# Layer A's instruction order from the planner: gate products behind the next chunk's first tile, weights loaded ahead of x

## The chip, the cores and the metric

The kernel runs on one core of a Trainium2 chip. Five engines with an instruction queue each matter here: TensorE (PE, matmuls; its weight loads are listed as PEld), VectorE (DVE), ScalarE (ACT), GpSimd (POOL) and SyncE (SP, which here only issues transfers). The metric is the device time of one execution in microseconds (us), the median of several runs.

## The reference, cut to what matters

A trunk of two layers on x with 2048 positions and 1024 channels, in float32. Layer A is a recurrent layer, layer B attention with a window of 128.

```python
def rglru_layer(x, norm_g, w_in, conv_w, conv_b, wr, br, wi, bi, lam, w_out):
    h = rmsnorm(x, norm_g)
    u = h @ w_in                                   # 1024 -> 2 x 1536
    xb, gate = u[..., :LRU_WIDTH], u[..., LRU_WIDTH:]
    xb = causal_depthwise_conv(xb, conv_w, conv_b) # 4 taps along the sequence
    xs = xb.reshape(bsz, seq, LRU_BLOCKS, LRU_BLOCK_W)       # 16 blocks of 96
    r = sigmoid(einsum('bshi,hij->bshj', xs, wr) + br)
    i = sigmoid(einsum('bshi,hij->bshj', xs, wi) + bi)
    log_a = -LRU_C * r * softplus(-lam)
    a = exp(log_a)
    b = sqrt(-expm1(2.0 * log_a)) * (i * xb)
    hs = associative_scan(a, b)                    # h = a * h_before + b
    return x + (hs * silu(gate)) @ w_out           # 1536 -> 1024
...
x = rglru_layer(x, ...)
k, v = ...                                         # from rmsnorm(x) @ w_kv
x = swa_layer(x, k, v, ...)                        # q and gate projection, attention, out-projection
```

## The kernel before

**Numbers.** Each float32 operand of a matmul is split into a high and a low float16 half with a power-of-two scale, and a product is three passes (high x high, high x low, low x high; `PASSES`). The scale of a weight comes from the maximum over all of it: DVE reduces the maxima, and two small PE products (`f2_turn`, `f2_back`, together called floor2) spread them over the partitions. So a weight is loaded, its maximum taken, and then ACT makes the high half and DVE the low half (`split_flat`, lines 310 and 311).

**Layer A.** Width 1536 is cut into four groups (g) of three tiles of 128 channels; the sequence into four chunks (c) of 512 positions. One group and one chunk make a *unit*; the 16 units run group by group, and are numbered here u = 4 g + c, from 0 to 15. A unit has 144 matmuls of 512 columns in the x-branch (`pu`, three tiles of 24 matmuls in three passes) and the gate branch (`pg`), and 36 for the two gates r and i (`pr`). Per x-branch tile, ACT makes a copy `u` and a first tap `xc`, DVE adds three taps (line 535), ACT and DVE or POOL split the result into `hl` (lines 537, 538), and SP copies 32 of its rows into `b3` (line 540; the profile calls it b), which the gate products read. ACT then works through four tables: SiLU of `pg` (line 548), sigmoid of `pr` (line 567) and tanh, exp, sqrt. DVE does the recurrence as a scan (line 592), multiplies by SiLU, and POOL's queue stores the result y in DRAM (`yD`, line 602).

**Where things come from.** All products share six PSUM banks in a ring ("mm"). For each x block of 128 positions ACT squares it and sums (line 326), POOL raises the sum to the power -0.5 (line 318), and ACT and DVE split. The blocks of chunk 0 are turned by PE (`turn_x`, line 333), those of chunks 1 to 3 by a transposing DMA on SP (`flip`, line 341). They come through three load buffers and three for the halves, which lie in the memory of two of the four weight buffers ("W") until the last block is done. Weights pass through three staging buffers ("st"). `prep(g)` loads and splits the weights of group g while group g - 1 runs. After the units come 16 blocks of the out-projection (`out_block`: load y and x, split y, 72 matmuls `po`, add, store to `x1D`), beside which layer B's weights are prepared (`prep_B`, `prep_out`).

**What sets the order.** The order is that of the program text, which the tile framework's scheduler changes by priorities. In the text `unit` is a generator that stops after each tile; at each stop `run_side` advances the side work (`norm_chunk` for x, `prep` for weights, `w_out_prep` for the out-projection) by a fixed number of steps (`RATE`), with offsets on the priority (`LATE`, `AHEAD`). In a unit the order of the products is: three x-branch tiles, three gate-branch tiles, the two gates' products.

Layer B is written otherwise. Its work is a set of chains, generators that name the engine and the duration of the next step before they issue it, or a flag to wait for. `Plan.run` plays all chains against each other at build time, always issues the step that can begin first (then by rank), and the order that results on each engine is fixed by ties from each instruction to the one before it:

```python
yield ACT_, 1150                       # engine, duration in ns
act.activation(hi, xb, AF.Copy, scale=r10)
yield DVE_, 1280, 1                    # 1: shares a port with POOL
dve.scalar_tensor_tensor(lo, xb, r10, hi, ALU.mult, ALU.subtract)
if b >= 2:
    yield F["proj"][b - 2]             # a flag
```

Of the kernel before, what the change touches and what calls it, by code (L numbers as in the profile page):

```python
# [46 lines left out]
RATE = (3, 3, 3, 2)  # L47
LATE = (0, 0, 0, 300, -100, 200)
F2AHEAD = 200
LO_POOL = (1, 2)  # L50
AHEAD = (200, 200, 200)
# [5 lines left out]
ACT_, DVE_, POOL_, SP_ = range(4)  # L57
# [15 lines left out]
class Plan:  # L73
# [5 lines left out]
    def __init__(self):  # L79
        self.now = 0.0  # L80
        self.free = [0.0] * 4
        self.port = [0.0] * 4
        self.table = None
        self.asks = []
        self.n = 0
# [4 lines left out]
    def step(self, chain, rank, t):  # L90
# [13 lines left out]
        elif r is not None:  # L104
            self.n += 1
            self.asks.append((t, rank, self.n, chain, r))
# [13 lines left out]

    def run(self, streams):
        heads = [next(s, None) for s in streams]
        pe = 0.0
        while True:
            best = None
# [5 lines left out]
            ask = min(self.asks, key=lambda a: (self.begin(a), a[1], a[2]), default=None)  # L131
            if best is None and ask is None:
                break
            if ask is None or best is not None and best[0] <= self.begin(ask):
                t, i = best
                pe = t + heads[i][1]
                self.now = pe + (170 if heads[i][1] else 0)
                heads[i] = next(streams[i], None)
                continue
# [3 lines left out]
            if r[0] is not None:  # L143
# [6 lines left out]
                end += WAKE  # L150
            self.step(ask[3], ask[1], end)
# [4 lines left out]
def trunk(ctx, tc, x, wA, gw, par, gains, woA, wkv, wB, woB, vec, alib, out):  # L156
# [62 lines left out]
    def floor2(mx, n, keep):  # L219


        with tc.high_priority(offset=F2AHEAD):
            dve.tensor_copy(keep, f2_back(f2_round(f2_turn(mx, n), n), n))

    def floor2_apart(mx, n, keep, t1, t2):
# [14 lines left out]
    lastmm = [None]  # L240

# [10 lines left out]

    def conv_bounds():
        cabs = xp.tile([P, KR, 5], F32, name="cabs")
        dve.scalar_tensor_tensor(cabs, pr[:, :, 0:5], -1.0, pr[:, :, 0:5], ALU.mult, ALU.max)
        csum = xp.tile([P, KR], F32, name="csum")
        dve.tensor_reduce(csum, cabs[:, :, 0:4], AX.X, ALU.add)
        cmx = xp.tile([P, 2], F32, name="cmx")
        dve.tensor_reduce(cmx[:, 0:1], csum, AX.X, ALU.max)
        dve.tensor_reduce(cmx[:, 1:2], cabs[:, :, 4], AX.X, ALU.max)  # L260
        floor2(cmx, 2, cb2)

    def decay():

        nlam = xp.tile([P, KR], F32, name="nlam")
        lamv = pr[:, :, 7]
        dve.tensor_scalar(nlam, lamv, -1.0, None, ALU.mult)
        nal = xp.tile([P, KR], F32, name="nal")
        dve.tensor_tensor(nal, nlam, lamv, ALU.min)
        ee = xp.tile([P, KR], F32, name="ee")  # L270
        act.activation(ee, nal, AF.Exp)
        e2 = xp.tile([P, KR], F32, name="e2")
        dve.tensor_scalar(e2, ee, 2.0, None, ALU.add)
        e3 = xp.tile([P, KR], F32, name="e3")
        dve.reciprocal(e3, e2)
# [1263 lines left out]
```

## Time and profile before

| what | us |
|---|---|
| median of 3 runs (lowest, highest) | 1579.13 (1576.9, 1579.64) |
| the profiled execution's own time | 1580.0 |
| its span, from the first to the last instruction | 1578.3 |
| PE busy | 1510.0 (96%) |
| DVE, ACT, POOL busy | 1049.3, 881.2, 460.2 |
| mean granted clock of PE | 0.986 |

By stage: unit 0 begins its matmuls at 19.9 us and unit 1 at 74.06, the units end at about 652, the out-projection ends at 910.46, and layer B takes the rest. The profile names an operation by its line; all large matmuls are issued at line 246, so that they are told apart by what they write (`pu`, `pg`, `pr`, `po` in layer A; `pm`, `s` and again `po` in layer B). A matmul row's busy time is modelled and overlaps its neighbours, so matmul counts are priced by the time from one to the next in a long unbroken run.

### The profile page before, as it was taken

How to read it: one execution, taken by the hardware profiler on the slowest of the kernel's cores; microseconds unless marked ns; L12 is line 12 of the kernel's file. 1: busy time of each engine (PE TensorE's matmuls, PEld its weight loads, DVE VectorE, ACT ScalarE, POOL GpSimd, SP SyncE). 2: the span in 40 equal slices, each digit the busy share in tenths (PEclk: the TensorE clock that was granted, in tenths of full speed). 3: DMA queues.
4: the chain of work that ended last, by engine and by line, in shares of the span. 5: the costliest groups of instructions: out<-in, count | busy, mean ns of one | idle time of the engine just before them, and what ended most of it. 6: DMA issues, size and time to landing. Idle time of an engine off the chain costs nothing.

```text
span 1578.3 us, 23221 instructions
## 1 busy us (share of the span) xinstructions
PE 1510.0 (96%) x8575; PEld 752.1 (48%) x8575; DVE 1049.3 (66%) x2221; ACT 881.2 (56%) x1771; POOL 460.2 (29%) x578
## 2 busy tenths in 40 slices
PE   5889999999989999889999998999999999999987
PEld 4434444444434444334444455555555555555553
DVE  7667868866886666766256246666666666767675
ACT  5767667766666566620144145655555656556661
POOL 2243222222222232100000033444444444444431
PEclk9999999999999999999999999999999999999998
DMA  6663302100341120779358343454444444444333
GB/s 202 168 145 75 102 28 86 58 26 26 110 163 43 40 86 26 243 262 329 131 194 295 108 101 57 84 97 98 97 98 97 97 98 98 97 97 96 72 68 94
DMA packets 242546, 177.29 MB, mean 112 GB/s; under 512 B 205056, under 2 KB 215552, under 8 KB 242432
## 3 DMA queue, kind: packets, MB, share of 16 engines
q1 hardware_dynamic: 233984, 146.95, 35.9%
q0 software_dynamic: 8304, 28.84, 5.3%
q8 instruction: 67, 1.10, 0.3%
q14 instruction: 47, 0.39, 0.1%
q10 hardware_dynamic: 144, 0.01, 0.0%
HBM read 92.93 MB, written 29.36 MB: 77 GB/s over the span
## 4 chain that ended last, share of the span: by engine, by line
PE 81%; DVE 7%; DMA 5%; ACT 3%; issue 2%; POOL 1%; SPq 0%; ACTq 0%; POOLq 0%; DVEq 0%
PE pm L246 33%; PE po L246 17%; PE pu L246 13%; PE pg L246 11%; PE pr L246 4%; PE s L246 3%; DVE xc L535 1%; DMA wst<-in_woA_dram 1%; DMA xs<-in_x_dram 1%; DMA ppx<-gg 1%; DVE w L311 1%; DMA xnT<-in_wkv_dram 1%; DVE h L592 1%; DVE amx L299 0%; DVE ri L589 0%
## 5 line engine op out<-in xcount | busy, mean ns | idle before, releaser
L246 PEld LDWEIGHTS <-w 128*128 128x128 f16 x2520 | 234.1, 98 | 279.5 <-issue 17.6
L246 PE MATMUL pm<-wq,xT 128*128 128x512 f16 x1536 | 351.8, 379 | 0.0
L246 PE MATMUL pu<-xnT,w 128*128 128x512 f16 (+1 forms) x1368 | 258.7, 349 | 8.2 <-ACT ri L567 7.2
L246 PEld LDWEIGHTS <-xT 128*128 128x128 f16 x1920 | 187.4, 98 | 163.8 <-issue 0.7
L246 PE MATMUL po<-wo,xnT 128*128 128x512 f16 x1152 | 252.9, 382 | 6.2 <-DVE wo L311 5.2
L246 PE MATMUL pg<-xnT,w 128*128 128x512 f16 x1152 | 253.3, 379 | 2.8 <-ACT w L310 1.9
L246 PEld LDWEIGHTS <-xnT 128*128 128x128 f16 x1152 | 113.3, 98 | 144.5 <-issue 11.5
L246 PE MATMUL pm<-xnT,yT 128*128 128x512 f16 x768 | 173.4, 381 | 0.0
L535 DVE SCALAR_TENSOR_TENSOR xc<-u,cwS,xc 128x512 f32<-128x512 f32 x144 | 119.8, 835 | 29.2 <-ACT xc L533 27.9
L1326 ACT ACTIVATE sq<-sq,bi,ssc 128x128 f32<-128x128 f32 x256 | 124.0, 486 | 22.8 <-DVE bi L1323 22.8
L246 PEld LDWEIGHTS <-yT 128*128 128x128 f16 x768 | 74.5, 98 | 85.9 <-issue 1.9
L1310 DVE CUSTOM_DVE_ANT_0 sq<-sq,al 128x128 f32<-128x128 f32 x256 | 99.4, 433 | 1.6
L1301 DVE COPY_PREDICATED sq<-mask,s 128x256 f32<-128x256 int32 x128 | 56.5, 442 | 48.5 <-ACT sq L1299 47.5
L537 ACT CAST hl<-xc 128x512 f16<-128x512 f32 x48 | 29.5, 614 | 99.5 <-DVE xc L535 99.4
L310 ACT ACTIVATE xnT<-xnT,sy 128x1536 f16<-128x1536 f32 x16 | 25.0, 1571 | 105.9 <-PE po L246 105.9
L1299 ACT COPY sq<-s 128x256 f32<-128x256 f32 x128 | 47.5, 372 | 64.2 <-PE s L246 63.4
L587 DVE SCALAR_TENSOR_TENSOR ri<-xc,isig,ri 128x512 f32<-128x512 f32 x48 | 33.3, 749 | 72.6 <-ACT ri L567 72.6
L246 PE MATMUL s<-kT,qT 128*128 128x256 f16 x512 | 77.7, 275 | 1.6 <-DVE qy L1385 0.9
L246 PE MATMUL pr<-hl,gw 128*128 128x512 f16 x288 | 70.7, 390 | 7.1 <-ACT gs L548 7.1
L567 ACT ACTIVATE ri<-pr,pr,rsc 128x512 f32<-128x512 f32 x96 | 67.2, 775 | 16.2 <-PE pr L246 16.1
L530 POOL COPY uhist<-u 128x3 f32<-128x3 f32 x36 | 14.4, 401 | 210.4 <-ACT u L524 210.3
L1385 DVE TENSOR_TENSOR qy<-qy,po 128x256 f32<-128x256 f32 x64 | 26.8, 421 | 67.8 <-ACT qy L1383 67.6
(245 smaller groups left out, 2252.4 us busy)
## 6 DMA issues: line engine op xcount, KB each, us to landing
xnT<-in_wB_dram SPq DMA_DIRECT2D x32, 512.0 KB, 6.4
yD<-gs POOLq DMA_DIRECT2D x48, 256.0 KB, 2.7
wst<-in_woA_dram SPq DMA_DIRECT2D x24, 512.0 KB, 4.5
xnT<-yD SPq DMA_DIRECT2D x16, 768.0 KB, 5.3
st<-in_wA_dram SPq DMA_DIRECT2D x15, 768.0 KB, 5.0
xs<-in_x_dram SPq DMA_DIRECT2D x16, 512.0 KB, 4.6
xnT<-in_x_dram SPq DMA_DIRECT2D x16, 512.0 KB, 4.6
x1D<-xnT POOLq DMA_DIRECT2D x16, 512.0 KB, 4.6
```

What stands on the lines that cost most here:

```text
L246: lastmm[0] = pe.matmul(o, lhsT, rhs, start=start, stop=stop, skip_group_check=True)
L310: act.activation(hi, src, AF.Copy, scale=scale)
L311: dve.scalar_tensor_tensor(lo, src, scale, hi, ALU.mult, ALU.subtract)
L535: dve.scalar_tensor_tensor(xc, u[:, d : d + CH], cw[:, j, d : d + 1], xc, ALU.mult, ALU.add)
L537: act.copy(hl[:, 0], xc)
L567: act.activation(v, o[j], AF.Sigmoid, bias=pr[:, t, 5 + w : 6 + w], scale=W["rsc"])
L587: dve.scalar_tensor_tensor(i, xs[j], W["isig"], i, ALU.mult, ALU.mult)
L1299: act.copy(sl, o[:, :, P:])
L1301: dve.copy_predicated(sl, mask.unsqueeze(1).to_broadcast([P, 2, P]), o[:, :, 0:P])
L1310: dve.tensor_tensor_reduce(s[:, h], s[:, h], al[:, i * P : (i + 1) * P], 1.0, -3.4e38, ALU.add, ALU.max, m)
L1326: act.activation(s[:, h], s[:, h], AF.Exp, bias=d["bi"][:, h : h + 1], scale=ssc[:, h : h + 1], accum_out=d["lsum"][:, h : h + 1],)
L1385: dve.tensor_tensor(yv, yv, o[:, :, 0], ALU.add)
```

## The change

Layer A and the first two blocks of the out-projection become chains of one plan; layer B's chains are kept. What an instruction computes stays, and their number too. In parts:

- *The plan.* `Plan` gets PE as a fifth engine, so that the small floor2 products are asked for like other steps, a model of landing times (2.3 us and 2.7 ns per KB, one after another), and a choice by begin time plus 30 ns per rank in which a switch of ACT's table counts nothing. At its end every instruction is tied to the one before it on its engine. `high_priority`, `RATE`, `LATE` and `AHEAD` are gone from layer A.
- *Order of products.* A unit is: x-branch tile 0, then the gate products of the unit before it, x-branch tiles 1 and 2, then the gate branch. The last unit's gate products stand after its gate branch.
- *The head.* The two halves of group 0's x-branch weights are loaded first, then x blocks 0 to 3, then the parameters and the second weights. Unit 0's x-branch is computed in three pieces of x blocks (0), (1) and (2, 3), three tiles at a time, where it was four pieces of one block, and each product waits for its own half of x and its own weight slice.
- *x of chunks 1 to 3.* One chain normalizes the twelve blocks one after another; loads wait for the buffer of the block three before.
- *Weights.* `prep` of groups 1, 2, 3 begins at units 2, 5 and 8, and that of the out-projection at unit 11 (`PREP_AT`). A split is a step per slice on ACT that starts a step on DVE. Out-projection weights are loaded one ahead.
- *Out-projection.* Blocks 0 and 1 are in the plan. Layer B's preparation runs beside blocks 2 to 15, where it ran beside blocks 1 to 15.

```diff
+PREP_AT = (2, 1, 0, 3)
+FIRST = ((0, 1), (1, 2), (2, 4))
+OUT_PLANNED = 2
+WEIGHT = 30
+TABLE = 0
+RANKA = (2, 6, 6, 4, 5, 6, 2, 3, 4, 4, 6, 6)
...
+    def landing(kb):
+
+        t = max(plan.now + 2300, plan.dma) + kb * 2.7
+        plan.dma = t
+        return t - plan.now
...
+    def split_steps(src, scale, hi, lo, hif, lof, ns, rank):
+        yield ACT_, ns
+        act.activation(hi, src, AF.Copy, scale=scale)
+        hif.set()
+        plan.go(split_lo(src, scale, hi, lo, lof, ns), rank)
...
+    def products():
+        for u in range(NTRI * NCH):
+            g, c = divmod(u, NCH)
+            W = WS[g]
+            un = units[u]
+            yield [W["set0"]] + xn_f[c], 0
+            unit_f[u].set()
+            if u == 0:
+                o, fr = yield from proj_first(W)
+                for j in range(3):
+                    plan.go(inx(un, j, o[j], fr[j]), RANKA[0])
+            else:
+                for j in range(3):
+                    o, free = yield from proj(W, 0, j, c, "pu")
+                    plan.go(inx(un, j, o, free), RANKA[0])
+                    if j == 0:
+                        yield from gates(units[u - 1])
+            if c == NCH - 1:
+                W["free0"].set()
+            yield [W["set1"]], 0
+            for j in range(3):
+                un.pg[j] = yield from proj(W, 1, j, c, "pg")
+                un.pg_f[j].set()
+            if c == NCH - 1:
+                W["free1"].set()
+        yield from gates(units[-1])
+        for b in range(OUT_PLANNED):
+            yield from out_products(b)
...
+    def ring_loads():
+        for p in range(NB - 4):
...
+                yield xfree[p - 3]
+            yield SP_, 450
+            load_x(1 + p // 4, p % 4, xb0[X_RING[p % 3]])
...
+    def norm_chain():
+        for p in range(NB - 4):
...
+            yield xload[p]
+            xb, t = xb0[X_RING[p % 3]], xb0[HL_RING[p % 3]].bitcast(F16)
+            hi, lo = t[:, 0:D], t[:, D : 2 * D]
+            r10 = yield from norm_steps(xb, lo)
+            yield ACT_, 1150
+            act.activation(hi, xb, AF.Copy, scale=r10)
+            yield DVE_, 1285, 1
+            dve.scalar_tensor_tensor(lo, xb, r10, hi, ALU.mult, ALU.subtract)
+            xfree[p].set()
+            plan.go(norm_flip(p, c, b, t), RANKA[7])
...
+    begin_plan()
+    plan.go(first_weights([Fetch([P, 4, 384], wsrc(0, 0, h), 0) for h in range(2)]), FIRST_RANK[0])
+    plan.go(first_loads(), 1)
...
+    plan.run([products()])
+    end_plan()
...
-    for b in range(NB):
+    for b in range(OUT_PLANNED, NB):
         for _ in out_block(b):
-            run_side(side, 2 if b else 0, LATE[5])
+            run_side(side, 2, LATE5)
```

More of the change, by code (lines that the diff above doesn't have):

```diff
@@ new lines, in trunk, with take @@
+    py, sy, cA = (xp.tile([P, NCH], F32, name=n) for n in ("py", "sy", "cA"))
+    plan = Plan(True, WEIGHT, TABLE)
+    flag = lambda: Flag(plan)
+    rings = {}
+    BUFS = dict(W=4, st=3, mm=6, tp=2, u=3, xc=4, hl=4, b3=2, gs=4, ri0=4, ri1=4, q=3, h=2, gw=2, f2=1)
+    def take(tag):
+        r = rings.setdefault(tag, [])
+        f = None
+        while len(r) >= BUFS[tag] and r[-BUFS[tag]] is not f:
+            f = r[-BUFS[tag]]
+            yield f
+        r.append(flag())
+        return r[-1]
@@ new lines, in together, with floor2_steps @@
+    def together(flags, then):
+        for f in flags:
+            yield f
+        then.set()
+    def floor2_steps(mx, n, keep, slack=300):
+        lock = yield from take("f2")
+        free = yield from take("tp")
+        if slack:
+            yield None, slack
+        yield PE_, 160
+        tp = f2_turn(mx, n)
+        yield DVE_, 700
+        dg = f2_round(tp, n)
+        free.set()
+        free = yield from take("tp")
+        if slack:
+            yield None, slack
+        yield PE_, 300
+        bp = f2_back(dg, n)
+        yield DVE_, 170
+        dve.tensor_copy(keep, bp)
+        free.set()
+        lock.set()
@@ new lines, in first_turn @@
+    def first_turn(b, w, src, fl):
+        free = yield from take("tp")
+        tp = pst([P, KD, P], F16, "tp", uniq("xt"), BUFS["tp"])
+        yield PE_, 620
+        for k in range(KD):
+            pe.transpose(tp[:, k], src[:, k * P : (k + 1) * P], id16)
+        dest = xnV[0][:, w, :, b * P : (b + 1) * P]
+        if w == 0:
+            yield ACT_, 1000
+            act.copy(dest, tp)
+        else:
+            yield DVE_, 690
+            dve.tensor_copy(dest, tp)
+        free.set()
+        fl.set()
+        (x_lo if w else x_hi)[b].set()
@@ L750, in trunk @@
-    drain(w_out_prep(3))
-    dve.tensor_scalar(cA[:, 0:2], py[:, 0:2], pwo, 2.0**-28, ALU.mult, ALU.mult)
+        wo_scaled.set()
+        for k, ld in enumerate(wo_loads(rank)):
+            if k % 3 == 0:
+                yield from take("W")
+                wo.append(wtile(uniq("wo")).rearrange("p a (k c) -> p a k c", k=3))
+            yield ld.landed
+            w, lo = wo[-1], wo_f[k]
+            yield from split_steps(ld.t, swo, w[:, 0, k % 3], w[:, 1, k % 3], flag(), lo, WO_NS, RANKA[10])
+            plan.go(together([lo], ld.free), 0)
@@ L792, in out_block, with ahead @@
         pool.dma_start(x1D[b], xb)
+    def ahead(loads, n):
+        q, loads = [], list(loads)
+        for _ in range(len(loads)):
+            while len(q) <= n and loads:
+                q.append(loads.pop(0)())
+            yield q.pop(0)
     stg = [0]
```

961 lines of the change are left out of this document (606 added, 355 removed).

## The prediction

> **What bounds it now.** First the page's busy times, then the busy time of each engine by stage (columns: stretch, length, busy us and instructions of PE, PEld, DVE, ACT, POOL, then granted clock, DMA share, GB/s):
>
> ```profile
> PE 1510.0 (96%) x8575; PEld 752.1 (48%) x8575; DVE 1049.3 (66%) x2221; ACT 881.2 (56%) x1771; POOL 460.2 (29%) x578
> ...
> 0.00:20.00 20.00, 3.71 (x29) 3.24 (x30) 11.55 (x30) 11.99 (x17) 5.46 (x21) 1.00 0.86 318
> 20.00:45.80 25.80, 21.65 (x335) 20.32 (x333) 22.94 (x69) 15.65 (x26) 4.00 (x10) 1.00 0.54 133
> 45.80:74.06 28.26, 22.42 (x109) 8.79 (x110) 19.25 (x34) 20.32 (x31) 7.33 (x13) 1.00 0.54 131
> 110.50:124.00 13.50, 5.66 (x21) 1.68 (x20) 1.52 (x2) 8.35 (x12) 2.16 (x7) 0.66 0.96 198
> ...
> 197.76:345.58 147.82, 147.82 (x729) 65.19 (x728) 110.73 (x177) 97.59 (x143) 39.18 (x50) 1.00 0.17 52
> 345.58:419.00 73.42, 73.42 (x362) 32.53 (x363) 52.77 (x88) 49.47 (x72) 18.46 (x25) 1.00 0.17 51
> 419.00:463.55 44.55, 40.54 (x193) 17.14 (x185) 36.65 (x56) 26.12 (x39) 11.24 (x15) 0.92 0.38 125
> ...
> 610.60:652.00 41.40, 38.44 (x190) 16.93 (x188) 33.32 (x47) 30.86 (x39) 10.59 (x8) 0.98 0.33 106
> 652.00:690.00 38.00, 32.29 (x136) 13.82 (x135) 30.35 (x40) 18.84 (x23) 2.79 (x4) 0.93 0.74 243
> 690.00:910.46 220.46, 220.46 (x1025) 100.09 (x1024) 103.90 (x116) 52.33 (x48) 8.52 (x17) 1.00 0.62 219
> 910.46:1578.30 667.84, 646.37 (x4225) 359.56 (x4222) 442.97 (x1301) 381.26 (x1086) 273.15 (x304) 0.99 0.43 91
> ```
>
> PE is the bound: 96% of the span, and where it never idles two units (a unit is one group g and one chunk c) take 73.42 us, 36.7 each. So a gain can only come from PE's idle time: 1578.3 - 1510.0 = 68.3 us, of which 667.84 - 646.37 = 21.5 lie in layer B, whose chains keep their order. The rest, 46.8, lies in six places: 16.3 before 20 us, 4.2 and 5.8 in unit 0, 7.8 in unit 1, 4.0 in unit 10, 3.0 in unit 15 and 5.7 at the start of the out-projection. Idle PE also runs on slowly (clock 0.66, 0.92, 0.93 in those rows), so the full loss of a place is its length less its matmuls at full rate.
>
> The timeline shows what those waits end on (start, length, engine and line, in brackets the idle time before and its releaser):
>
> ```profile
> 4.25 1.06 ACT L326 ACTIVATE xri<-xs 128x1024 bf16<-128x1024 f32 x1 [1.73 <-DMA xs<-in_x_dram]
> 9.72 1.06 ACT L326 ACTIVATE xri<-xs 128x1024 bf16<-128x1024 f32 x1 [1.85 <-DMA xs<-in_x_dram]
> 11.99 0.37 PE L200 MATMUL f2t<-id,m 128*1 128x128 f32 x1 [11.99 <-DVE m L407]
> ...
> 74.06 2.29 PE L246 MATMUL pu<-xnT,w 128*128 128x512 f16 x5 [4.05 <-ACT ri L567]
> ...
> 111.54 1.06 ACT L326 ACTIVATE xs<-xs 128x1024 bf16<-128x1024 f32 x1 [4.25 <-DMA xs<-in_x_dram]
> 115.74 1.44 PE L246 MATMUL pr<-hl,gw 128*128 128x512 f16 x3 [4.64 <-ACT gs L548]
> ...
> 457.16 1.47 PE L246 MATMUL pr<-b,gw 96*32 96x512 f16 x9 [4.01 <-DMA b<-hl]
> ...
> 651.94 13.64 SPq L809 DMA_DIRECT2D xnT<-in_wB_dram  x6
> 674.20 4.50 SPq L674 DMA_DIRECT2D wst<-in_woA_dram  x3
> 674.22 10.27 PE L246 MATMUL po<-wo,xnT 128*128 128x512 f16 x39 [4.92 <-DVE wo L311]
> ```
>
> In the head the weights' maximum comes last (11.99). In unit 1 ACT sat 4.25 us before the square of an x block whose load was late; SiLU stood behind it in ACT's queue and held a PSUM bank, and the gate products waited 4.64. In unit 10 they waited 4.01 for the copy of b. At 674 the out-projection waited 4.92 for its last weights, whose loads were issued at 674.20 behind layer B's loads on SP.
>
> **The change, step by step.** Prices per instruction:
>
> ```profile
> L310 ACT ACTIVATE w<-st,gs 128x384 f16<-128x384 f32 x60 | 32.4, 607 | 6.9 <-DVE gs L305 6.9
> L326 ACT ACTIVATE xri<-xs 128x1024 bf16<-128x1024 f32 x4 | 4.2, 1048 | 3.6 <-DMA xs<-in_x_dram 3.6
> L310 ACT ACTIVATE xri<-xs,r 128x1024 f16<-128x1024 f32 x4 | 4.6, 1146 | 3.2 <-POOL r L320 3.2
> L299 DVE TENSOR_REDUCE amx<-st 128x4 f32<-128x1536 f32 x15 | 26.2, 1749 | 14.8 <-DMA st<-in_wA_dram 14.8
> L335 ACT COPY xnT<-xt 128x1024 f16<-128x1024 f16 x4 | 4.0, 1002 | 0.9 <-PE xt L333 0.8
> L524 ACT COPY u<-pu 128x512 f32<-128x512 f32 x48 | 27.6, 575 | 2.4 <-PE pu L246 2.4
> L533 ACT ACTIVATE xc<-pu,cwS 128x512 f32<-128x512 f32 x48 | 37.5, 782 | 0.0
> L537 ACT CAST hl<-xc 128x512 f16<-128x512 f32 x48 | 29.5, 614 | 99.5 <-DVE xc L535 99.4
> L548 ACT ACTIVATE gs<-pg,gsc 128x512 f32<-128x512 f32 x48 | 32.7, 682 | 54.1 <-PE pg L246 54.0
> L548 ACT ACT_TABLE_LOAD x16 | 20.5, 1283 | 0.3
> 155.04 5.51 PE pr L246 x36
> 809.13 101.33 PE po L246 x469
> xnT<-xs SPq DMA_TRANSPOSE x12, 5.3
> ```
>
> *Head, weights before x.* The removed order put x block 0 first on SP, then two weight halves, then x blocks 1 to 3. Between 4.25 (block 0 landed) and 9.72 (block 1) two halves of 768 KB and one x block of 512 KB landed: 2048 KB in 5.47 us. At that rate, and with block 0 now third, I estimate the halves at 4.9 and 7.0, the blocks at 8.4, 9.7, 11.1 and 12.5. DVE reduces the second half from 7.0 to 8.8 (1.75), and with the small reductions behind it the maximum is there at about 9.3 instead of 11.99, so the split can start before the last x blocks are in. ACT then sets the pace: four blocks at 1.05 + 1.15 (8.8), four copies at 1.0 (4.0), eight weight slices at 0.607 (4.9): 17.7 us from 8.4, so 26.1, with bubbles 28. The three pieces of the first tile (blocks 0, 1, and 2 with 3) leave 72 matmuls of 256 columns for after that: half of the 512-column 0.216 (101.33 / 469) each, 7.8 us, so 36. The gate-branch projections add 72 x 0.216 = 15.6: 51.5.
>
> Unit 1 needs chunk 1 normalized. ACT must also do the second weights (4.9), the convolution side of three tiles (3 x (0.575 + 0.782 + 0.614) = 5.9), four more blocks (8.8) and three SiLUs with a table load (3.3): 22.9 more, so 8.4 + 17.7 + 22.9 = 49.0 without any wait; the last block's low half and flip (5.3) come behind. I take 57 for the start of unit 1. Before it was 74.06, which included unit 0's gate products; those (5.5) now come behind unit 1's first tile, so compare 68.5. Gain 11.5. Ends: 17 (PE alone, 51.5) and 0 (ACT no denser than now: 36.0 busy of 54.1 between 20 and 74).
>
> *Units 1 and 2.* They took 160.55 - 74.06 = 86.5 us (the chain's 155.04 + 5.51 ends unit 2) for 73.4 of work: 13.1 lost. Now the planner interleaves loads, norms and tables, and SiLU need not stand behind a load. But ACT works 97.59 / 4 = 24.4 us in a unit, and four blocks add 8.8: 33.2 of 36.7. That leaves little room, so I keep 4 us of loss: gain 9, ends 0 and 13. The next group's weights now load from unit 2 on instead of in unit 0, which takes 3.5 MB off SP and the DMA engines while x comes in. Their splits (16 x 0.607 = 9.7 on ACT) need the buffers that hold x until the last norm, so they fall into unit 3 and have until unit 4 for the first half and one x-branch (15.6) longer for the second; if they slip past that, PE waits for them and each us counts. Price 0.
>
> *Gate products behind the next first tile.* No work is removed; PE reaches them 20.8 us after the last conv tile instead of 15.6, so the 4.01 wait of unit 10 is covered by the 5.2 of a tile. What waits behind them in PE's order is the next tiles 1 and 2. A bank is the new danger: tile 1 takes the bank that the first sigmoid frees, so ACT must do it within the 2.75 us of the second gate's products. Unit 10 loses 44.55 - 36.7 = 7.85; I take 7, ends 4 and 7.8. Four of the units between run at 147.82 / 4 = 37.0 now: 0.
>
> *Unit 15 and the out-projection.* Unit 15 loses 41.4 - 36.7 = 4.7; PE stood while ACT, whose queue it needed, worked only 2.89 of 4.30 us (first row of the last table below). In the plan a weight split asks for ACT only when its load has landed. I take 3, ends 0 and 4.7. The out-projection takes 910.46 - 652 = 258.5 for 16 x 72 x 0.216 = 248.8: 9.7 lost, nearly all before 690. Blocks 0 and 1 and the last weight loads are now inside the plan, their loads one ahead. Outside it layer B's preparation may still slip its loads in between on SP; so 5, ends 0 and 8.
>
> *Layer B.* Its preparation starts at block 2 instead of 1, one block (15.6 us) later; its last split was at 870.5, 40 us before the end:
>
> ```profile
> L311 DVE SCALAR_TENSOR_TENSOR xnT<-ws,swb,xnT x8: 1276/1284/1286, 811.0 to 870.5; 128x1024 f16<-128x1024 f32 x8
> ```
>
> Price 0, covered by the out-projection. If it started two blocks later and ended 31 us later, 9 us of cover would still be left; beyond that each us counts whole.
>
> *New waits.* Every instruction of an engine is now tied to the one before it in the plan, 16 gate products and some twenty small transpositions among PE's. Where the chip is later than the plan, PE stands. Nearest row: layer B, ordered this way already, whose 21.5 us idle in 668 hold also its start and its end. I take 3, ends 0 and 10 (half of that).
>
> Such a wait costs more than its length:
>
> ```profile
> 645.00:649.30 4.30, 1.84 (x15) 0.60 (x7) 3.33 (x3) 2.89 (x4) 0.00 (x0) 1.00 1.01 386
> 649.30:651.40 2.10, 1.59 (x12) 0.52 (x12) 0.70 (x1) 2.09 (x3) 0.00 (x0) 0.84 0.84 242
> 651.40:654.00 2.60, 2.60 (x7) 0.92 (x7) 0.61 (x1) 2.60 (x5) 0.00 (x0) 0.50 0.82 235
> ```
>
> PE was idle 2.46 us, then 0.5, and the clock stood at 0.50 for the next 2.6 us, 1.3 us lost on top. The Trainium skill (TensorE: Matmul & The Clock Gate, Part 1) has the clock halved only after an idle window of about 3.4 us; by it a wait of 2.5 us would be free of that, and the 3 us taken here would shrink by 1.3, the time to about 1546. The trace disagrees, at least for two idles close together, and I keep the trace's price.
>
> **Sum.** 11.5 + 9 + 7 + 3 + 5 - 3 = 32.5. The profiled execution took 1580.0 (1578.3 span and 1.7 around it): 1580.0 - 32.5 = 1547.5. The median of the runs, 1579.13, is 0.9 lower, so 1547. All good ends give 17 + 13 + 7.8 + 4.7 + 8 = 50.5, 1529; all bad ones 4 - 10 = -6, 1586.
>
> **Rivals.**
> 1. ACT becomes the bound of units 1 and 2. Its 33.2 us fit only if it hardly waits; in order, with one late load or sum, it keeps all 13.1 and half the head is lost too (6): 6 + 0 + 7 + 3 + 5 - 3 = 18, 1562. For: ACT already did 36.0 of 54.1 in unit 0. Against: the order is made with those durations in view.
> 2. Slower: the supply of normalized x. One chain now takes the blocks one after another (square, POOL's power, high half, low half: 1.05 + 1.15 on ACT, POOL's and DVE's parts between), with three load buffers, and the flips share SP with everything. With t per block from 26 us on and 6 for the last flip, unit 3 starts at 32 + 12 t. Without its moved gate products it started at 155. The other terms give 12, so it decides at 32 + 12 t = 167, t = 11.3 us; at t = 11.8 the kernel takes 1586. Against: the blocks came every 8.4 us before (12 squares, row below), which gives 133, only some 3 us late. For: in unit 1 the DMA engines were 0.96 busy at 198 GB/s, mostly with these loads and flips.
>
> ```profile
> L326 ACT ACTIVATE xs<-xs x12: 1040/1048/1080, 26.1 to 118.5; 128x1024 bf16<-128x1024 f32 x12
> ```
>
> 3. The change doesn't do what it says: the waits move along the same queues, and gains and new waits cancel; 1579.
>
> **Chances.** The forecast (1534 to 1560) 0.62; rival 1 (1560 to 1574) 0.19; better than 1534 0.03; no change 0.05; slower by rival 2 or by another mishap of its kind 0.11. The time named is that of the likeliest. From 1534 to 1574 the range leaves out 0.03 below and 0.16 above. Faster by over 0.2%, about what a measurement of this kernel can tell from no change, 0.84; within it 0.04; slower 0.12.
>
> **What would show it.** Head: the first transposition of a maximum near 9.4, unit 0's x tiles done by 36, unit 1 begun by 57. Units: starts 36.7 apart from unit 1 on, no PE wait on SiLU or on b, ACT near 0.9 busy in units 1 and 2. Gate products between tiles 0 and 1, no PE wait on a sigmoid there. End: no PE wait on wo; layer B at 667 to 669 us. Wrong it would be if unit 3 starts later than 140, if PE stands on the small transpositions, or if layer B starts late on its weights.

## The result and the profile after

| | before | after |
|---|---|---|
| median of the runs (lowest, highest), us | 1578.02 (1574.82, 1579.64) | 1541.14 (1539.6, 1542.53) |
| span of the profiled execution | 1578.3 | 1540.8 |
| PE, ACT, POOL busy | 1510.0, 881.2, 460.2 | 1498.6, 882.3, 414.8 |

The median before is now that of four runs. The ratio is 0.977, 95% interval 0.975 to 0.979: 36.9 us gone, where 32.5 were forecast. PE's idle time fell by 26.1 of the 37.5 us of span (68.3 to 42.2), and its busy time by 11.4, at a mean granted clock of 0.993 where it was 0.986. The three pieces of unit 0 also make 72 small matmuls fewer (8575 to 8503), so the number of PE's instructions did change. The stretches of the changed kernel, cut where its stages begin (same columns as before):

```profile
15.00:58.23 43.23, 38.58 (x344) 26.77 (x343) 39.16 (x101) 33.68 (x53) 8.40 (x24) 1.00 0.59 159
58.23:94.92 36.69, 36.69 (x180) 16.15 (x181) 20.35 (x27) 30.30 (x44) 12.35 (x22) 1.00 0.52 127
94.92:133.94 39.02, 37.50 (x185) 16.57 (x184) 31.50 (x48) 30.83 (x44) 13.71 (x26) 1.00 0.56 145
393.20:429.90 36.70, 36.70 (x181) 16.11 (x180) 26.82 (x41) 26.02 (x39) 7.10 (x15) 1.00 0.21 67
577.39:621.70 44.31, 42.52 (x210) 18.35 (x208) 29.88 (x44) 32.03 (x40) 7.26 (x12) 0.98 0.34 109
623.64:873.50 249.86, 249.86 (x1163) 113.44 (x1161) 130.09 (x152) 66.32 (x66) 11.36 (x21) 1.00 0.63 220
873.50:1540.80 667.30, 645.17 (x4225) 359.43 (x4222) 445.57 (x1301) 381.15 (x1086) 277.75 (x304) 0.99 0.44 91
```

PE is without a gap in unit 1 (36.69 of 36.69), in unit 10 and at the start of the out-projection, three of the six places that held the idle time. What is left of layer A's idle time lies ahead of 58 us, in unit 2 (1.5) and at the end of unit 15 (1.8). The timeline shows what those waits end on; all large matmuls are now issued at line 274:

```profile
5.66 1.75 DVE L415 TENSOR_REDUCE amx<-st 128x4 f32<-128x1536 f32 x1 [2.54 <-DMA st<-in_wA_dram]
10.24 0.37 PE L220 MATMUL f2t<-id,m 128*1 128x128 f32 x1 [10.24 <-DVE m L516]
...
58.23 2.10 PE L274 MATMUL pu<-xnT,w 128*128 128x512 f16 x9 [1.98 <-DMA xnT<-xs]
...
101.85 0.69 ACT L733 ACTIVATE gs<-pg,gsc 128x512 f32<-128x512 f32 x1 [7.88 <-DMA yD<-gs]
104.78 1.46 PE L274 MATMUL pr<-hl,gw 128*128 128x512 f16 x6 [1.06 <-ACT xc L670]
...
619.86 2.72 PE L274 MATMUL pr<-hl,gw 128*128 128x512 f16 x6 [1.79 <-ACT gs L733]
```

The groups by line show the wait behind the last three rows:

```profile
L733 ACT ACTIVATE gs<-pg,gsc 128x512 f32<-128x512 f32 x48 | 32.9, 688 | 94.0 <-DMA yD<-gs 70.1 <-DVE ymx L809 15.6 <-PE pg L274 6.4
```

This row groups all 48 SiLUs (count, busy, mean ns, idle time before them and what ended it): ACT stood 70.1 us ahead of them for a y store to land, since a `gs` buffer is free only then. That wait is new; it reaches PE twice, in unit 2 (1.06 us, for the convolution that stood behind a SiLU on ACT) and in unit 15.

Where the 37.5 us of span came from, by the starts of the units in the two timelines: head 68.5 - 58.2 = 10.3; units 1 and 2 86.5 - 75.7 = 10.8; unit 10 44.1 - 36.7 = 7.4; unit 15 with its moved gate products taken off 40.8 - 40.9 = -0.1; out-projection, from its first matmul (651.4 and 623.64), 259.1 - 249.9 = 9.2; layer B 667.8 - 667.3 = 0.5; the units between, 405.9 - 406.5, -0.6.

### The profile page after: what moved, and what is told of

It reads as the page before. It is cut to its first block, busy times and chain, and to the rows that moved or that the text cites. A ratio compares the mean times of both kernels' runs of the same rounds, so it can differ in the third digit from the quotient of the medians.

```text
span 1540.8 us, 23049 instructions
## 1 busy us (share of the span) xinstructions
PE 1498.6 (97%) x8503; PEld 748.6 (49%) x8503; DVE 1054.5 (68%) x2221; ACT 882.3 (57%) x1771; POOL 414.8 (27%) x578
## 3 DMA queue, kind: packets, MB, share of 16 engines
q1 hardware_dynamic: 233984, 146.95, 36.9%
## 4 chain that ended last, share of the span: by engine, by line
PE 91%; DVE 3%; DMA 3%; ACT 2%; issue 1%; POOL 0%; SPq 0%; ACTq 0%; DVEq 0%; POOLq 0%
PE pm L274 33%; PE po L274 19%; PE pu L274 16%; PE pg L274 14%; PE pr L274 5%; PE s L274 4%; DMA yD<-gs 1%; DMA qT<-qy 1%; DMA ppx<-gg 1%; ACT sq L1754 0%; DMA xnT<-xs 0%; DMA st<-in_wA_dram 0%; POOL gg L1778 0%; PE f2b L236 0%; DVE ri L787 0%
## 5 line engine op out<-in xcount | busy, mean ns | idle before, releaser
L274 PE MATMUL pu<-xnT,w 128*128 128x512 f16 (+2 forms) x1296 | 258.8, 358 | 2.9 <-DMA xnT<-xs 2.0
L274 PE MATMUL po<-wo,xnT 128*128 128x512 f16 x1152 | 249.4, 379 | 0.0
L674 DVE SCALAR_TENSOR_TENSOR xc<-u,cwS,xc 128x512 f32<-128x512 f32 x144 | 110.7, 776 | 68.4 <-ACT xc L670 65.2
L274 PEld LDWEIGHTS <-yT 128*128 128x128 f16 x768 | 74.4, 98 | 85.8 <-issue 1.7
L684 POOL TENSOR_TENSOR hl<-xc,hl 128x512 f16<-128x512 f32 x32 | 42.2, 1321 | 174.3 <-ACT hl L679 135.3
L733 ACT ACTIVATE gs<-pg,gsc 128x512 f32<-128x512 f32 x48 | 32.9, 688 | 94.0 <-DMA yD<-gs 70.1
L1727 ACT COPY sq<-s 128x256 f32<-128x256 f32 x128 | 47.5, 372 | 59.4 <-PE s L274 58.2
L1201 DVE SCALAR_TENSOR_TENSOR xnT<-po,cA,xnT 128x512 f32<-128x512 f32 x28 | 20.8, 747 | 70.3 <-PE po L274 70.3
L815 POOL DMA_DIRECT2D yD<-gs x48 | 36.9, 768 | 118.5 <-DVE gs L805 118.3
```

Of the source, the lines that this page charges most:

```text
L274: lastmm[0] = pe.matmul(o, lhsT, rhs, start=start, stop=stop, skip_group_check=True)
L674: dve.scalar_tensor_tensor(xc, u[:, d : d + CH], cw[:, j, d : d + 1], xc, ALU.mult, ALU.add)
L684: (pool if j in LO_POOL else dve).tensor_tensor(hl[:, 1], xc, hl[:, 0], ALU.subtract)
L733: act.activation(gs, o, AF.Silu, scale=W["gsc"])
L815: pool.dma_start(yD[4 * c : 4 * c + 4, :, t, :].rearrange("b p n -> p b n"), gs.rearrange("p (b n) -> p b n", n=P),)
L1201: dve.scalar_tensor_tensor(xs_, o[n], cA[:, c : c + 1], xs_, ALU.mult, ALU.add)
```

## The experiments

My theory after the result: the gain is an order on the in-order queues made with the landing of loads in view. The rivals are the single edits of the change: weights ahead of x, the moved gate products, the planned out-projection blocks. This table has where the stages begin in each profiled run (us); the text below quotes it. In the kernel before, e1 and e6 unit 0's gate products (5.5) lie ahead of unit 1, in all others behind its first tile:

| kernel | unit 1 | unit 3 | unit 10 | unit 11 | out-projection | median time |
|---|---|---|---|---|---|---|
| before | 74.1 | 160.5 | 419.4 | 463.5 | 651.4 | 1578.0 |
| after | 58.2 | 133.9 | 393.2 | 429.9 | 623.6 | 1541.1 |
| e9 no ties | 64.0 | 144.3 | 420.7 | 457.4 | 651.8 | 1572.6 |
| e4 landing at once | 67.9 | 143.6 | 403.0 | 439.7 | 641.6 | 1562.5 |
| e1 gates at their own unit | 69.6 | 148.6 | 408.3 | 446.6 | 632.3 | 1551.4 |
| e5 before, gates moved | 74.4 | 157.4 | 426.2 | 468.3 | 663.3 | 1589.7 |
| e6 before, weights first | 73.5 | 161.4 | 420.3 | 464.4 | 652.5 | 1577.0 |
| e2 x block 0 first | 68.2 | 145.9 | 405.3 | 442.0 | 634.4 | 1554.4 |
| e2b, POOL in one step | 69.2 | 149.5 | 408.9 | 445.6 | 637.9 | 1556.8 |
| e2d, norms ahead | 61.0 | 136.9 | 396.3 | 433.0 | 625.2 | 1545.9 |
| e12 after, norms ahead | 59.8 | 135.6 | 395.0 | 431.7 | 625.3 | 1545.2 |
| e8 weights of group 1 early | 62.0 | 145.9 | 405.2 | 441.9 | 634.2 | 1552.4 |
| e3 out blocks not planned | 61.3 | 138.6 | 397.9 | 434.6 | 628.5 | 1543.5 |
| e7 a fifth gs buffer | 58.0 | 135.4 | 396.5 | 433.1 | 624.9 | 1543.0 |

**The order itself.** e9 keeps the chains, the buffers and the loads, and drops the ties:

```diff
-    begin_plan()
...
-    end_plan()
```

> The changed kernel with layer A's chains, buffers and loads as they are, but without the ties that hold each engine to the order of the plan, so that the scheduler of the framework orders the instructions of DVE, ACT, POOL and SP by its own costs. Theory O: the order is where the gain of units 1, 2 and 10 and of the head comes from; the time goes back to 1555 to 1575, with PE waits of several us on ACT in the first three units. Rival C: the chains' data, buffers and the load order carry the gain, and the ties only fix what would come out anyway: 1541 to 1546.

Measured 1572.6 (ratio to before 0.996, 0.994 to 0.997): 31 of the 37 us are lost again. Its largest group of PE's waits up to the out-projection (engine, line and releaser; total, times, longest), and DVE and PE around one of them:

```profile
PE f2b L236 <- DVE f2d L231: 17.3, 4, 6.5
```

```profile
282.05 0.27 DVE L225 TENSOR_REDUCE f2m<-f2t 1x1 f32<-1x128 f32 x1
282.88 0.69 DVE L785 SCALAR_TENSOR_TENSOR q<-ri,q 128x512 f32<-128x512 f32 x1 [0.56 <-ACT q L759]
283.49 0.13 DVE L227 TENSOR_SCALAR f2n<-f2m 1x1 f32<-1x1 f32 x1
283.61 0.69 DVE L787 TENSOR_TENSOR ri<-ri,q 128x512 f32<-128x512 f32 x1
284.22 0.13 DVE L229 TENSOR_SCALAR f2o<-f2n 1x1 uint32<-1x1 uint32 x1
284.28 0.73 DVE L674 SCALAR_TENSOR_TENSOR xc<-u,cwS,xc 128x512 f32<-128x512 f32 x1
284.94 0.20 DVE L231 TENSOR_SCALAR f2d<-id,f2o 1x1 f32<-1x1 f32 x1
285.19 0.58 PE L236 MATMUL f2b<-f2d,ones 1*128 1x1 f32 x2 [5.09 <-DVE f2d L231]
```

The four small steps behind a maximum (L225 to L231) are 0.7 us of work, but the framework's order puts one large DVE operation between each two, and PE, which has the second small product next in its order, stands 5.1 us. Such waits of 4.66, 5.09 and 6.46 lie in units 0, 6 and 9.

The table says where the loss is, and it bears theory O out only in part. Unit 10 takes 36.7 here as in the changed kernel, so that all its 7.4 are there without the ties. So are 7.7 of the 9.2 in the out-projection (651.8 to 903.2 in the trace), 6.2 of the 10.8 in units 1 and 2 (80.3 instead of 86.5) and 4.5 of the 10.3 in the head (64.0 against 68.5). What eats them up is units 3 to 9: 276.4, where the kernel before takes 258.9 and the changed one 259.3. So the chains, their buffers and loads bring most of the gain in those places; the ties bring the rest of the head and of units 1 and 2, some 10 us, and keep the small products from losing 17 us that the kernel before never lost.

**The landing in the plan.** e4 lets the plan believe that every load lands 0.1 us behind its issue:

```diff
-        t = max(plan.now + 2300, plan.dma) + kb * 2.7
+        t = plan.now + 100
```

> The changed kernel with a plan that believes every load of weights and x lands 0.1 us after its issue; the program's instructions are the same, only their order differs. Theory A (before the change units 1 and 2 and the tail lost time because ACT and DVE, in order, stood in front of work whose load was late, and the modelled landing keeps them from it): ACT and DVE wait on loads again, PE behind them, 1551 to 1565. Rival (any order by chains is good enough, the margins hide it): 1540 to 1545.

Measured 1562.5 (0.990, 0.989 to 0.991), 21 us more than the changed kernel and within theory A's range. The timeline of DVE and PE in its head, and of PE in unit 11:

```profile
15.07 1.75 DVE L415 TENSOR_REDUCE amx<-xs 128x4 f32<-128x1536 f32 x1 [5.27 <-DMA xs<-in_wA_dram]
17.03 0.37 PE L220 MATMUL f2t<-id,m 128*1 128x128 f32 x1 [17.03 <-DVE amx L417]
...
468.11 0.37 PE L220 MATMUL f2t<-id,m 128*1 128x128 f32 x1 [4.50 <-DVE m L1054]
```

In the head DVE took the maximum of the second weights, which it believed there, ahead of the step that closes the first maximum, and stood 5.27 us for the load; PE began at 17.03, not 10.24. In unit 11 PE stood 4.50 for the maximum over the out-projection's weights, whose loads were late. Where an order is fixed, a load that the plan takes to be there holds all that is behind it.

**The moved gate products.** e1 puts them back behind their own gate branch; all else stays planned:

```diff
-                    if j == 0:
-                        yield from gates(units[u - 1])
...
-        yield from gates(units[-1])
+            yield from gates(un)
```

> The changed kernel with each unit's gate products directly behind its own gate branch again, everything else in the plan. Theory A (four separate places, each freed by the planned order; the displaced gate products only give margin): the plan still keeps loads, norms and splits out of ACT's way, so PE meets the gate products 15.6 us after the last conv tile with little waiting: 1541 to 1550, 1545 likeliest, single waits of 1 to 3 us on b or on SiLU. Theory B (the displacement itself removes the waits on the gate products): the 10.7 of units 1 and 2 and the 7.4 of unit 10 come back: 1559 or more.

Measured 1551.4 (0.983, 0.982 to 0.985), 10 us slower than after and between the ranges of the two theories. Unit 0 with its own gate products ends at 69.6, against 58.2 + 5.5 = 63.7, so 5.9 later; units 1 to 3 take 3.7 more, units 9 to 11 3.1 more, and unit 15 4.2 less. About 3 us of unit 0 are no wait but a slow clock (its gate branch ended at 59.2, not 56.25; last section). Without them some 7 of the 10 are left for the edit; as even the run of e1 with the highest mean clock (0.994) took 1550.6, it may be up to 9.

In unit 10 I had put the gain down to the moved products. SP and PE there, first of this kernel, then of the kernel before:

```profile
420.13 17.78 SPq L691 DMA_DIRECT2D b<-hl  x3
437.95 6.00 SPq L382 DMA_DIRECT2D st<-in_woA_dram  x4
441.44 0.83 PE L274 MATMUL pr<-b,gw 96*32 96x512 f16 x9
```

```profile
452.24 0.33 SPq L674 DMA_DIRECT2D wst<-in_woA_dram  x1
452.62 0.51 SPq L540 DMA_DIRECT2D b<-hl  x1
451.04 2.11 PE L246 MATMUL pr<-hl,gw 128*128 128x512 f16 x9
```

Before, the third copy of b stood on SP behind a weight load and was issued at 452.62, after the gate products had begun. Of the wait of 4.01, about 0.8 comes from the convolution itself (POOL finished that `hl` at 452.03), 0.6 from SP's order, and 2.6 from the landing: 4.5 us behind the weight load, where the other four copies of b between 400 and 470 us took 1.9 to 2.9. In e1 all three copies are issued by 437.95, ahead of four weight loads, and the product with b follows at 441.44 with no wait. Unit 10 takes 38.3 there, against 44.1: 5.8 of the 7.4 us come without moving a product.

e5 does the reverse: the kernel before, with everything from the gate products on issued behind the next unit's first tile.

```diff
+            if j == 0 and held[0]:
+                held[0]()
...
+        def finish():
+            r = gate(0)
...
+        held[0] = finish
```

> The kernel before with one part of the change alone: the gate products and what follows them are issued behind the next unit's first x-branch tile; order otherwise by the scheduler. Theory A: unit 10's wait on b (4.0, with the slow clock 7.4 lost) and unit 15's part vanish, the waits behind late x loads in units 1 and 2 stay at least in part: 1566 to 1574, 1570 likeliest. Theory B: all waits on the gate products vanish, 18 us and more: 1560 or less.

Measured 1589.7: slower than before (1.007, 1.006 to 1.009), and outside both ranges. PE no longer waits for b in unit 10, which gains 2.0 (42.1); a tile between is enough for that too. But other places lose more. The two largest waits of PE up to the out-projection:

```profile
PE f2t L200 <- DVE m L407: 18.6, 4, 12.5
PE pu L246 <- issue: 9.2, 1, 9.2
```

Of the first, 12.5 is the start of the head, as in the kernel before (12.0); the other 6.1 are waits for a weight's maximum in units 3, 6 and 10. The second stands ahead of unit 1, which begins at 74.4 as before: the gate products that filled part of that wait now come behind it, and the head is 5.9 longer (74.4 against 68.5). Units 3 to 9 take 268.8 instead of 258.9. So the same displacement costs 12 us in the framework's order and brings 7 to 9 in the planned one.

**The head.** e6 is the kernel before with the two weight halves loaded ahead of x block 0:

```diff
-    load_x(0, 0, xb0[0])
...
-    for b in range(1, CH // P):
+    for b in range(CH // P):
```

> The kernel before with one part alone: the two weight halves of group 0 loaded ahead of x block 0. Theory A: the maximum is ready some 2 to 3 us earlier, but unit 1 starts when chunk 1 is normalized, which this does not touch: 1576 to 1579. Rival (the loads' order carries the head): 1568 to 1571.

Measured 1577.0: no change (0.9995, 0.9985 to 1.0005). The first small product came at 10.1 there, against 12.0 before, but unit 1 at 73.5: the last flip of chunk 1 was issued at 67.86 and landed 5.5 us later, at 73.4, so that chunk 1's x sets it. e2 is the reverse, the changed kernel with x block 0 ahead of the weights:

```diff
+    def first_x():
+        yield SP_, 450
+        load_x(0, 0, xb0[0])
...
-        for b in range(CH // P):
+        for b in range(1, CH // P):
...
+    plan.go(first_x(), -1)
```

> The changed kernel with x block 0 loaded ahead of the two weight halves, the other three blocks behind them, as before the change. Theory A (in the head ACT's 17.7 us of work set the pace, and weights first only lets it start early): the weights' maximum comes 1.4 us later (one x block at 2.67 us per MB), ACT squares block 0 meanwhile; unit 1 starts 0 to 2 us later: 1541 to 1543. Rival (the head's 10 us come from the order of these loads): unit 1 starts 6 to 10 us later, 1547 to 1551.

Measured 1554.4 (0.985, 0.984 to 0.986), 13 us slower and 3 above the rival's range. POOL's timeline, where the block that unit 1 waits for is normalized:

```profile
48.65 0.57 POOL L909 TENSOR_TENSOR rs<-var,mhalf 128x1 f32<-128x1 f32 x1
57.15 2.66 POOL L684 TENSOR_TENSOR hl<-xc,hl 128x512 f16<-128x512 f32 x2 [7.93 <-ACT hl L679]
59.90 0.22 POOL L912 TENSOR_SCALAR r<-rs 128x1 f32<-128x1 f32 x1
```

The power was done at 49.22; the scale behind it, 0.22 us long, came at 59.90, because two low halves of `hl` stood between them in the order and POOL waited 7.93 us for ACT. e2b takes that away by making the three POOL operations of a norm one step of the plan:

```diff
-        yield POOL_, 190, 1
+        yield POOL_, 985, 1
...
-        yield POOL_, 575
...
-        yield POOL_, 220, 1
```

> The changed kernel with x block 0 loaded first, as in the run before with 1554.4, but POOL's three small steps of a block's normalization (sum, power, scale) are one step of the plan, so that nothing can be put between them. Theory P (the 13 us of that run were one in-order stall: the plan put two subtractions of unit 0 on POOL in front of the last scale of chunk 1, and on the chip they stood 7.9 us): unit 1 starts at 58 to 61 instead of 68.2 and the kernel takes 1542 to 1547. Rival (the load order itself costs it): unit 1 near 68, 1552 to 1556.

Measured 1556.8 (0.987, 0.985 to 0.988): no gain, and theory P is out. On POOL no step of chunk 1's norms stands behind the low halves any more, but ACT and DVE now hold the same block:

```profile
51.45 0.22 POOL L910 TENSOR_SCALAR r<-rs 128x1 f32<-128x1 f32 x1
59.45 2.17 DVE L1018 SCALAR_TENSOR_TENSOR xs<-xs,r 128x1024 f16<-128x1024 f32 x1
59.00 3.63 POOL L684 TENSOR_TENSOR hl<-xc,hl 128x512 f16<-128x512 f32 x2 [7.33 <-ACT hl L679]
```

The scale is there at 51.67, but ACT made the block's high half at 54.06, behind three first taps of unit 0's convolution, and DVE its low half at 59.45, behind the nine operations of that convolution. So e2d holds the convolution of unit 0 instead until chunk 1's low halves are issued:

```diff
+        if g == 0 and c == 0:
+            for f in x1low:
+                yield f
         un.xf[j], xc = yield from take_p1("xc", [P, CH])
...
             xfree[p].set()
+            if p < 4:
+                x1low[p].set()
```

> The changed kernel with x block 0 loaded ahead of the weights, and the convolution of unit 0 not begun (on ACT and behind it on DVE and POOL) until the four blocks of chunk 1 have their low halves. Theory S: in the two kernels before it with x block 0 first, the last block of chunk 1 came behind unit 0's convolution on one in-order engine, POOL in the first, DVE in the second, and that alone put unit 1 at 68.2 and 69.3. With the order turned round, its square stays near 47 us, its low half comes near 52, its flip lands near 58, and unit 1 begins between 58.5 and 60.5; the time is 1554.4 less 8 to 10, so 1544 to 1547. Rival U: the later weights themselves are the cause (the split of the second weights frees the load buffer of the third block later), and the order is only what is seen behind it: unit 1 stays at 65 us or later and the time at 1551 to 1557.

Measured 1545.9 (0.979, 0.977 to 0.980), 8.5 less than e2, and unit 1 at 61.0, a little later than the 60.5 expected. DVE's low half and PE:

```profile
53.99 1.28 DVE L1024 SCALAR_TENSOR_TENSOR xs<-xs,r 128x1024 f16<-128x1024 f32 x1 [3.13 <-ACT xs L1022]
61.05 5.34 PE L274 MATMUL pu<-xnT,w 128*128 128x512 f16 x24 [2.07 <-issue]
```

Theory S holds: two thirds of what the load order seemed to cost was unit 0's convolution standing ahead of one block of chunk 1, on POOL in e2, on ACT and DVE in e2b. What is left for the load order itself is 4.7 against the changed kernel (1545.9 and 1541.1), but only 0.7, with overlapping intervals, against e12 below, which holds the convolution in the same way. Which of the two is nearer isn't shown.

e12 makes e2d's edit of the convolution (the diff above) in the changed kernel, as a candidate for a better version.

> The changed kernel with weights ahead of x as it is, and the convolution of unit 0 held until the four blocks of chunk 1 have their low halves. Theory S: there the last block's low half stands ahead of the convolution already (51.07 us), so the edit moves nothing on the path: unit 1 at 57.5 to 58.5, time 1540 to 1543. Rival: the convolution that is now a little later reaches the gate products behind unit 1's first tile too late and PE waits there, 1544 to 1548; or the last flip comes 1 to 2 us earlier and 1539 is reached.

Measured 1545.2 (0.978, 0.977 to 0.980), 2 above theory S's range, and its interval overlaps that of the changed kernel. Nothing was won: the low half stood ahead of the convolution already, and PE waited 2.00 for the flip, as in the changed kernel (1.98). The time lies in the rival's range, but its late gate products are not to be seen. The profiled run is late by 1.6 us at unit 1 through a slow clock between 28 and 32 us (last section). Its runs go with the mean clock, 1542.5 at 0.994 and 1544.8 to 1547.8 at 0.991 and 0.992, which speaks for the same in most of them.

e8 lets group 1's weights load and split from unit 0 on:

```diff
-PREP_AT = (2, 1, 0, 3)
+PREP_AT = (0, 1, 0, 3)
```

> The changed kernel with the loads and splits of group 1's weights allowed from unit 0 on, as they were before, instead of from unit 2 on. Theory X: 3.5 MB more pass through SP and the DMA engines, and 9.7 us more of splits through ACT, while x comes in; units 1 and 2 lose 4 to 8 us: 1545 to 1549. Rival: the load buffers hold x until the last norm, so the weights can't start much earlier, and the plan puts them where there is room: within 1.5 us of the changed kernel, 1540 to 1542.5.

Measured 1552.4 (0.983, 0.981 to 0.985): 11 lost, more than theory X's 4 to 8. Unit 1 began at 62.0 and took 47.1:

```profile
46.88 1.75 DVE L415 TENSOR_REDUCE amx<-st 128x4 f32<-128x1536 f32 x1 [0.21 <-DMA st<-in_wA_dram]
60.64 2.12 ACT L670 ACTIVATE xc<-pu,cwS 128x512 f32<-128x512 f32 x3 [5.02 <-DVE cwS L485]
```

DVE took the maximum over group 1's weights at 46.88, and their floor2 went ahead of that of the convolution's scales. Those came at 60.6, ten us later than in the changed kernel, ACT began the convolution at 60.64, and the gate products behind unit 1's first tile then waited for b (1.47) and for SiLU (1.88). About 2 us of the 11 may be the slow clock of the last section; the late start of the next weights then carries some 9 us.

**Two small ones.** e3 takes the out-projection blocks out of the plan:

```diff
-OUT_PLANNED = 2
+OUT_PLANNED = 0
...
-            run_side(side, 2, LATE5)
+            run_side(side, 2 if b else 0, LATE5)
```

> The changed kernel with no block of the out-projection in the plan; layer B's preparation again runs beside blocks 1 to 15. Theory A (the two planned blocks keep layer B's loads from slipping in front of the last out-projection weights): a wait on wo or on the y loads of 3 to 7 us comes back after unit 15: 1545 to 1549. Rival (the weights loaded one ahead inside the plan, which stays, did it): 1540 to 1543.

Measured 1543.5 (0.978, 0.977 to 0.980), just above the rival's range. From the start of the out-projection to the end its profiled run takes 1545.9 - 628.5 = 917.4, the changed kernel 1540.8 - 623.6 = 917.2: the planned blocks are worth nothing. What the term gained is seen on ACT and DVE of the kernel before, ahead of the 674.22 at which PE went on:

```profile
662.66 3.21 ACT L310 ACTIVATE wo<-wst,swo 128x1024 f16<-128x1024 f32 x3
665.14 1.28 DVE L588 SCALAR_TENSOR_TENSOR q<-ri,q 128x512 f32<-128x512 f32 x2
672.89 1.28 DVE L311 SCALAR_TENSOR_TENSOR wo<-wst,swo,wo 128x1024 f16<-128x1024 f32 x1
```

Three high halves of the weights were done by 665.87, but DVE worked on the last unit's recurrence from 665.14 on and made the first low half at 672.89; the last one came at 684.96. In the changed kernel the last low half comes at 628.08, and PE meets no wait. Since e9 keeps most of this gain, the ties are not needed for it. Which part of the chains brings it is open; that the loads run one ahead isn't it by itself, as the kernel before had them two ahead.

e7 gives `gs` a fifth buffer:

```diff
-    BUFS = dict(W=4, st=3, mm=6, tp=2, u=3, xc=4, hl=4, b3=2, gs=4, ri0=4, ri1=4, q=3, h=2, gw=2, f2=1)
+    BUFS = dict(W=4, st=3, mm=6, tp=2, u=3, xc=4, hl=4, b3=2, gs=5, ri0=4, ri1=4, q=3, h=2, gw=2, f2=1)
```

> The changed kernel with five buffers instead of four for SiLU's result gs. Theory G (the displaced gate products keep gs in use longer, so SiLU waits until a store of y has landed, 70 us of ACT's idle time; PE stands behind it 1.06 us in unit 2 and 1.79 at the end, at the slow clock after that): these two places go, 1537 to 1539.5. Rival (SiLU's wait is off PE's path and another wait follows at once): 1540.5 to 1542.

Measured 1543.0 (0.978, 0.976 to 0.979), no gain, and above both ranges. SiLU's wait for y stores fell from 70.1 to 37.6, and the last unit with its gate products took 44.5 instead of 46.4; but the order changed with it, and unit 3 waited 2.0 us for a flip of x.

## Why the prediction came out, step by step

The sum is 4 to 5 us short of the measurement, and closer than its terms are. Units 1 and 2 and the out-projection were put 6 us too low and the new waits counted twice (3), the head and unit 15 were put 4 us too high. That these partly cancel is luck.

- *Head.* 11.5 forecast, 10.3 measured; the size held, the reason only in part. The first small product came at 10.24, not 9.4: the first half landed at 5.66, not 4.9, and DVE's two reductions of 1.75 then stood one behind the other. Unit 0's x tiles ended at 40.0, not 36: DVE's last copy of x block 3 into `xnT` was done at 32.5, where I had all of ACT's part done by 28, with the same 7.8 us of matmuls behind it. I had credited the weights' place; alone in the kernel before it brings nothing (e6), in the plan 0.7 to 4.7 (e2d). By e2, e2b and e2d the rest goes with chunk 1 being normalized ahead of unit 0's convolution; no run takes only that away.
- *Units 1 and 2.* 9 forecast, 10.8 measured, 2.3 of loss left instead of 4. ACT was busy 30.30 of 36.69 and 30.83 of 39.02, 0.83 and 0.79, not 0.9: with four squares of x in unit 1 and three in unit 2, and 2.2 for a block, that leaves 21.5 and 24.2 for the rest, where I had 24.4 and four blocks for both.
- *Unit 10.* 7 forecast, 7.4 measured, with half of the reason. A tile between does take the wait for b away (e5), as forecast; but 5.8 of the 7.4 come without it, because the plan finishes the convolution earlier and puts its copies ahead of the weight loads on SP (e1). Either is enough for the wait, and no PE wait on b is left.
- *Unit 15.* 3 forecast, -0.1 measured: the term of the sum that failed. The weight splits no longer hold ACT, but the last gate products now wait 1.79 us for a SiLU that waits for a y store. I had ruled out PE waits on SiLU and put no price on that buffer; the clock falls behind the wait:

```profile
618.00:620.00 2.00, 0.21 (x2) 0.10 (x1) 2.00 (x2) 0.84 (x2) 0.00 (x0) 0.97 0.79 231
620.00:622.00 2.00, 2.00 (x6) 0.61 (x4) 2.00 (x2) 1.97 (x3) 0.00 (x0) 0.50 0.97 268
```

  The stretch takes 46.4 where unit and products need 36.7 + 5.5 = 42.2: 1.8 of wait and about as much again of half clock, the price that the prediction took from 645 to 654 us of the kernel before. In e1 unit 15 with its own products, without that wait, takes 36.7.
- *Out-projection.* 5 forecast, 9.2 measured. What I took off for layer B's loads slipping in between on SP cost nothing: PE is busy for all of the 249.86 us. My reading of the wait was wrong, too. PE went on at 674.22, when the loads of 674.20 had only been issued; it had waited for a low half that DVE put behind the recurrence (rows at e3).
- *New waits.* 3 forecast. Within the units are 1.06 + 0.46 + 1.79 = 3.3, but they are already in the terms above, so that as a term of its own it was counted twice. They are not on the small transpositions (0.15 us in all behind the first maximum); 1.06 and 1.79 of them go back to SiLU's buffers.
- *Layer B.* 0 forecast, 0.5 measured. Its last weight split began at 846.6, 27 us ahead of its start.
- *Rivals.* ACT as the bound: no, by the shares above. Supply of x: unit 3 began at 133.94, which is t = 8.5 us per block by the formula there, not 11.3; but e2 and e2b show that this rival's mechanism is real: one block behind the convolution in the order, and unit 1 is 10 us late. No change: that is what weights ahead of x alone would have given (e6). In e9 gains and new waits nearly cancel, as that rival has it, once the ties are gone.
- *The clock's price.* The runs bear out the row, not the rule of the Trainium skill (last section): a wait of 1.79 us cost more than its length.
- *The bad end.* 1580.0 + 6 less the 0.9 is 1585, not 1586.

What is shown by runs: that the ties (e9), the landing model (e4), the moved products (e1), the late start of the weights (e8) and the place of one x block (e2d) each carry time in this kernel. They overlap: 31, 21, 7 to 9, some 9 and 8.5 are not to be added. What in the chains clears unit 10 and the out-projection without the ties is not separated.

## What to carry to other kernels

When engines run in a fixed order, price a change by what it puts in front of what: look in the timeline for a short operation whose input is long done (the scale of 0.22 us at 59.90) and read what stands ahead of it. A plan made ahead of time needs the landing times of loads as much as the durations of the instructions; without them it was worth 16 us here instead of 37. A run that loses a gain should be read place by place: e9 lost 31 us, but 17 of them where there had been nothing to gain. And an edit that is good in one order can cost in another (the moved gate products: 7 to 9 gained, 12 lost), so test it in the order in which it will run.

## What the runs showed of the hardware

The clock of PE fell with no long idle time. Two stretches of the changed kernel, then two of e3 (columns as in the windows above; the clock is third from the end):

```profile
24.00:28.00 4.00, 1.80 (x26) 1.39 (x24) 3.86 (x10) 2.55 (x5) 0.00 (x0) 1.00 0.26 94
28.00:30.00 2.00, 1.99 (x31) 1.86 (x31) 2.00 (x3) 1.01 (x2) 0.82 (x2) 1.00 0.20 78
```

```profile
24.00:28.00 4.00, 1.61 (x22) 1.17 (x20) 3.86 (x10) 2.16 (x4) 0.00 (x0) 0.91 0.20 54
28.00:30.00 2.00, 1.78 (x14) 1.67 (x15) 2.00 (x3) 1.21 (x3) 0.62 (x2) 0.50 0.39 158
```

From 24 to 28 us PE was busy 1.80 of 4 us in the changed kernel and kept its clock; in e3 it was busy 1.61, the clock fell to 0.50 until 34 us, and unit 1 came 3.1 us later. No single idle time in these two stretches is over 1.1 us. In the same 4 us e12, e8, e1 and e9 were busy 1.62, 1.59, 1.54 and 1.52 and lost the clock for 2 to 6 us, and e7, busy 2.06, kept it. So in these seven runs the lower busy share goes with the lost clock. A share or a length alone doesn't decide, though: with PE busy throughout ahead of the wait, the changed kernel kept its clock at 1.00 behind an idle time of 1.98 us at unit 1 and lost it behind one of 1.79 us in unit 15, and e7 lost it behind 2.01 us at unit 3; e6 lost it although it was busy 1.95 us from 20 to 24 us. What decides is open. The Trainium skill (TensorE: Matmul & The Clock Gate, Part 1) halves the clock after an idle window of about 3.4 us. These traces differ: the clock fell with PE idle for some 0.6 of 4 us in short pieces, and in unit 15 behind one idle time of 1.79 us.

POOL's large operations became shorter. The same 32, before and after:

```profile
L538 POOL TENSOR_TENSOR hl<-xc,hl 128x512 f16<-128x512 f32 x32 | 62.9, 1965 | 13.8 <-ACT hl L537 13.6
```

```profile
L684 POOL TENSOR_TENSOR hl<-xc,hl 128x512 f16<-128x512 f32 x32 | 42.2, 1321 | 174.3 <-ACT hl L679 135.3
```

1965 ns became 1321, and their sum fell by 20.7 of the 45.4 us that POOL's busy time lost. It isn't the ties that do it: in e9 the mean is 1354. That they now meet DVE's large operations less often is my explanation, which no run tests alone; where the two met in e2b, DVE's 1.28 us operation took 2.17 beside POOL's (59.45, row above). POOL's busy time is 27% of the span, and I count none of the 37 us as its gain.
